# A row-sum kernel's first load as two partition halves, issued by SyncE and ScalarE at the program's entry

## The chip, the cores and the metric

The kernel runs on one core of a Trainium2 chip. Times are device microseconds of one execution, without the profiler unless a text says "in its trace". Profiles come from one profiled execution, whose span runs from the first to the last instruction.

## The reference

The input is 67 MB of float32, and each row of 1024 numbers is summed.

```python
def setup_inputs():
    batch, seq, dim = 32, 512, 1024
    return {"x": np.random.randn(batch, seq, dim).astype(np.float32)}

def reference(x):
    return np.sum(x, axis=-1).astype(np.float32)
```

## The kernel before

The 16,384 rows are cut into eight groups of 16 rows for each of the 128 partitions. A group is 8.4 MB, 64 KB per partition, and is loaded into one of three buffers. SyncE issues all loads, so they stand in one queue (q1 of the page below, 67.12 MB). VectorE (DVE) sums the rows as they land. At the end ScalarE (ACT) helps with some of them. The first group is cut in two, 4 rows and 12 rows, so that DVE gets work early, and the first load is moved in front of the entry barrier. These are the parts that matter here:

```python
def issue_first_load_at_entry(nc):
    main, *rest = nc.main_func.blocks
    SP = mybir.EngineType.SP
    for block in rest:
        insts = list(block.instructions)
        at = next((k for k, i in enumerate(insts)
                   if isinstance(i, mybir.InstDMACopy) and i.engine == SP), None)
        if at is None:
            continue
        load = insts.pop(at)
        assert not load.sync_info.on_wait
        block.instructions = insts
        entry = list(main.instructions)
        k = next(k for k, i in enumerate(entry)
                 if isinstance(i, mybir.InstDrain) and i.engine == SP)
        main.instructions = entry[:k] + [load] + entry[k:]
        return

# ... (cut)
FIRST = 4
# ...
def rows(t, a, n, j, n_act):
    nv = n - n_act
    block = t[:, a * dim : (a + n) * dim].rearrange("p (n d) -> p n d", d=dim)
    load = nc.sync.dma_start(out=block, in_=rows_from(j, n))
    if nv:
        sums_of.append(vec(sums[:, j : j + nv], block[:, :nv, :]))
    # ... (cut: ScalarE's rows)
    return load

for g in range(last):
    t = inpool.tile([P, BIG * dim + 4], fp32)
    if g == 0:
        rows(t, 0, FIRST, 0, 0)
        first = sums_of[-1]
        rows(t, FIRST, BIG - FIRST, FIRST, 0)
        continue
    load = rows(t, 0, BIG, g * BIG, BIG // 2 if g == last - 1 else 0)
    if g == 1:
        hold(load, first, "no descriptors of later loads while the first ones start")
```

## Time and profile before

| | before |
|---|---|
| time, median of the 6 runs made beside the changed kernel | 162.57 us (162.22 to 163.04) |
| span of the profiled run | 160.4 us |
| first issue on SyncE | 0.00 to 0.38 us |
| first reduce starts | 7.19 us |
| 12-row reduce starts | 21.72 us |
| distance of the 16-row reduces | 19.35 us |
| first of the last row's three pieces landed (DVE waits for it; the last piece landed at 157.61) | 156.89 us |

The profile page of the kernel before has these lines: the span, each engine's busy time, and the load queue q1 with its packets, megabytes and share of sixteen DMA engines' time.

```profile
span 160.4 us, 125 instructions
...
DVE 121.1 (76%) x17; ACT 18.5 (12%) x33; POOL 0.2 (0%) x4
...
q1 hardware_dynamic: 2304, 67.12, 97.4%
```

The load stream is busy for nearly the whole span and DVE is not. The timeline of DVE shows the same. Its columns are start, duration, engine, line, operation, names, shapes, count, and in brackets the idle time before it and what ended it.

```profile
7.19 4.42 DVE L98 TENSOR_REDUCE sums<-t 128x4 f32<-128x4096 f32 x1 [7.19 <-DMA t<-in_x_dram]
21.72 12.95 DVE L98 TENSOR_REDUCE sums<-t 128x12 f32<-128x12288 f32 x1 [10.11 <-DMA t<-in_x_dram]
41.07 17.22 DVE L98 TENSOR_REDUCE sums<-t 128x16 f32<-128x16384 f32 x1 [6.40 <-DMA t<-in_x_dram]
60.42 17.22 DVE L98 TENSOR_REDUCE sums<-t 128x16 f32<-128x16384 f32 x1 [2.13 <-DMA t<-in_x_dram]
79.78 17.22 DVE L98 TENSOR_REDUCE sums<-t 128x16 f32<-128x16384 f32 x1 [2.14 <-DMA t<-in_x_dram]
99.13 17.22 DVE L98 TENSOR_REDUCE sums<-t 128x16 f32<-128x16384 f32 x1 [2.13 <-DMA t<-in_x_dram]
```

A 16-row reduce takes 17.22 us, and then DVE stands still for 2.1 us until the next load lands. The loads set the pace: 8.39 MB in 19.35 us is 433 GB/s.

The timeline of the entry shows SyncE's first two issues:

```profile
0.00 0.38 SPq L137 DMA_DIRECT2D t<-in_x_dram  x1
...
0.79 0.33 SPq L137 DMA_DIRECT2D t<-in_x_dram  x1
```

In the windows view, a row is a stretch: its length, the busy time of DVE, ACT and POOL, the clock, the mean busy share of the DMA engines, and GB/s. A packet counts where it starts, so short windows are uneven, and a share can exceed 1.

```profile
2.00:6.00 4.00, 0.00 (x0) 0.07 (x1) 0.00 (x0) 1.00 0.99 422
```

In this stretch all sixteen DMA engines are busy and move 422 GB/s. The trace also records every DMA packet, with its start, duration, size and queue but without its engine. The first load is 128 packets of 16 KB, so eight for each of sixteen engines if they are shared out evenly (at 3, 4 and 5 us sixteen are in flight). The first fourteen, started up to 1.32 us, take 0.94 to 1.43 us; from 2.4 us on, a packet takes 0.61 us (one of them 0.70).

### The profile page before, as it was taken

How to read it: one execution, taken by the hardware profiler on the slowest of the kernel's cores; microseconds unless marked ns; L12 is line 12 of the kernel's file. 1: busy time of each engine (PE TensorE's matmuls, PEld its weight loads, DVE VectorE, ACT ScalarE, POOL GpSimd, SP SyncE). 2: the span in 40 equal slices, each digit the busy share in tenths (PEclk: the TensorE clock that was granted, in tenths of full speed). 3: DMA queues.
4: the chain of work that ended last, by engine and by line, in shares of the span. 5: the costliest groups of instructions: out<-in, count | busy, mean ns of one | idle time of the engine just before them, and what ended most of it. 6: DMA issues, size and time to landing. Idle time of an engine off the chain costs nothing.

```text
span 160.4 us, 125 instructions
## 1 busy us (share of the span) xinstructions
DVE 121.1 (76%) x17; ACT 18.5 (12%) x33; POOL 0.2 (0%) x4
## 2 busy tenths in 40 slices
DVE  0280059960799959999499994999949998697882
ACT  3000000000000000000000000000000000696882
POOL 0000000000000000000000000000000000000000
DMA  7999996996996996996996996996999989999992
GB/s 261 458 466 515 392 523 261 523 523 261 523 523 261 523 523 261 523 523 261 523 523 261 523 523 262 523 490 294 523 392 392 523 360 425 392 425 425 407 399 61
DMA packets 3216, 67.18 MB, mean 419 GB/s; under 512 B 1296, under 2 KB 1680, under 8 KB 1808
## 3 DMA queue, kind: packets, MB, share of 16 engines
q1 hardware_dynamic: 2304, 67.12, 97.4%
q10 hardware_dynamic: 912, 0.06, 0.3%
HBM read 67.11 MB, written 0.07 MB: 419 GB/s over the span
## 4 chain that ended last, share of the span: by engine, by line
DMA 72%; DVE 25%; SPq 1%; issue 0%; DVEq 0%
DMA t<-in_x_dram 72%; DVE sums L98 24%; SPq L137 1%; DVE t L112 1%; DVEq L112 0%; DVEq L214 0%
## 5 line engine op out<-in xcount | busy, mean ns | idle before, releaser
L98 DVE TENSOR_REDUCE sums<-t 128x16 f32<-128x16384 f32 (+5 forms) x11 | 120.1, 10917 | 36.1 <-DMA t<-in_x_dram 36.1
L125 ACT ACTIVATE unread<-t 128x1024 f32<-128x1024 f32 x16 | 16.2, 1012 | 138.2 <-DMA t<-in_x_dram 138.2
L125 ACT ACTIVATION_READ_ACCUMULATOR unread<-t 128x1 f32 x16 | 3.0, 186 | 0.0
L112 DVE CUSTOM_DVE_ANT_0 t<-t 128x241 f32<-128x241 f32 (+2 forms) x3 | 1.0, 339 | 0.9 <-DMA t<-in_x_dram 0.7
L125 ACT ACT_TABLE_LOAD x1 | 1.3, 1283 | 0.8 <-PEq L203 0.8
L112 DVE DVE_READ_ACCUMULATOR2_ANT t<- 128x1 f32 x2 | 0.2, 84 | 0.0
L203 POOL MEMSET const-bfloat16-1.0<- 128x1 bf16 x1 | 0.1, 102 | 0.0
L203 POOL MEMSET const-uint8-127<- 128x1 uint8 x1 | 0.1, 102 | 0.0
L203 POOL MEMSET const-float32-0.0<- 128x1 f32 x1 | 0.1, 100 | 0.2 <-issue 0.2
L203 POOL MEMSET const-float32-1.0<- 128x1 f32 x1 | 0.1, 99 | 0.0
L112 DVE DVE_READ_ACCUMULATOR2_ANT sums<- 128x1 f32 x1 | 0.1, 83 | 0.0
## 6 DMA issues: line engine op xcount, KB each, us to landing
t<-in_x_dram SPq DMA_DIRECT2D x1, 6144.0 KB, 20.9
t<-in_x_dram SPq DMA_DIRECT2D x2, 2048.0 KB, 21.4
t<-in_x_dram SPq DMA_DIRECT2D x1, 4096.0 KB, 31.2
t<-in_x_dram SPq DMA_DIRECT2D x1, 1024.0 KB, 37.7
t<-in_x_dram SPq DMA_DIRECT2D x1, 512.0 KB, 38.5
t<-in_x_dram SPq DMA_DIRECT2D x1, 241.0 KB, 38.6
t<-in_x_dram SPq DMA_DIRECT2D x1, 144.0 KB, 38.6
t<-in_x_dram SPq DMA_DIRECT2D x1, 127.0 KB, 38.3
```

The source lines that it names most:

```text
L98: return nc.vector.tensor_reduce(out=dst, in_=src, axis=mybir.AxisListType.X, op=mybir.AluOpType.add)
L112: return nc.vector.tensor_tensor_reduce(out=src[:, :n], in0=src[:, :n], in1=src[:, n:], scale=1.0, scalar=0.0, op0=mybir.AluOpType.add, op ...
L125: nc.scalar.activation(out=unread[:, :n], in_=src, func=mybir.ActivationFunctionType.Copy, accum_out=dst,)
L137: load = nc.sync.dma_start(out=block, in_=rows_from(j, n))
L203: nc = _bacc.Bacc("TRN2", target_bir_lowering=False, num_devices=1)
```

## The change

The intent is to start the stream sooner: two queues each take half of the first load at the program's entry, instead of one queue taking all of it. Partitions 0 to 63 go to SyncE, partitions 64 to 127 to ScalarE.

```diff
+def issue_first_loads_at_entry(nc):
+    for engine in (mybir.EngineType.SP, mybir.EngineType.Activation):
+        issue_first_load_at_entry(nc, engine)
+
-def issue_first_load_at_entry(nc):
+def issue_first_load_at_entry(nc, SP):
     main, *rest = nc.main_func.blocks
-    SP = mybir.EngineType.SP
@@
-    nc.at_finalize(issue_first_load_at_entry)
+    nc.at_finalize(issue_first_loads_at_entry)
@@ def rows(t, a, n, j, n_act):
-            load = nc.sync.dma_start(out=block, in_=rows_from(j, n))
+            if j == 0:
+                half = P // 2
+                for eng, p0 in ((nc.sync, 0), (nc.scalar, half)):
+                    load = eng.dma_start(
+                        out=block[p0 : p0 + half], in_=rows_from(j, n)[p0 : p0 + half]
+                    )
+            else:
+                load = nc.sync.dma_start(out=block, in_=rows_from(j, n))
```

## The prediction

> **What bounds the kernel now.** The load stream. The page gives 67.11 MB read in a span of 160.4 us, queue q1 busy for 97.4% of sixteen engines' span; DVE is busy 76%, ACT 12%. The chain of waits is 72% DMA t<-in_x_dram. In the timeline the 16-row reduces start every 19.35 us (41.07, 60.42, 79.78, 99.13, 118.49), so 8.39 MB per 19.35 us = 433 GB/s, and DVE idles 2.1 us before each. All 67.11 MB at that rate is 155 us; the last load lands at 156.9. So only some 2 us in front of the stream and 3.5 us behind it are not bandwidth. The front: SyncE's first issue is 0.00 to 0.38, the first packets start at about 1.0 (windows view), the first reduce starts at 7.19. 2.10 MB at 433 GB/s is 4.84 us, so the stream starts, in effect, at 2.35.

> **What the change does.** The first load (2048 KB, 4 rows) becomes two of 64 partitions, one on each queue. Removed: at most part of SyncE's 0.38 us issue (estimate 0.05 to 0.15, later issues take 0.33) and perhaps some of the spread of the engines' first packets (first starts lie between 1.0 and 1.6). Added: one issue on ScalarE (its store's issue took 0.41), before its table load at 0.79; ScalarE first works on data at 137.8, so that is free. The second load's issue (0.79) may slip by 0.1 to 0.2 us; its packets are wanted only at 6.4. The first reduce waits for two semaphores. All else stays. Since the stream never runs dry afterwards, the end moves by exactly what the stream gains or loses in its first 10 us.

> **The gain** is at most 0.3 us (0.2%): after its first packet each engine is already at full rate[...].

> **The danger** is the shape. [...] Nothing in this trace shows it yet. [...] up to twice 4.84 us for the first 2.1 MB, a loss of up to 4.8 us. [...] I take a mean loss of about 1.3 us, and expect no gain over 0.5 us.

> **Predicted time:** 163.8 us, 8 in 10 between 162.2 and 167.3. Faster by over 2%: 0.01; within 2%: 0.72; slower by over 2%: 0.27.

> **What would show it.** The first reduce's start: 7.0 to 7.4 [...], 8.5 to 12 if not. The windows view between 2 and 7 us: about 430 GB/s, or 220 to 350. The start of the 12-row reduce (21.72) and of the 16-row ones, all shifted by one constant equal to the change of span; DVE's idle time before each 16-row reduce still 2.1 us. The span behind the last load unchanged at about 3.5 us.

> **What would make it wrong.** The low half finishing first, so that 48 KB packets of the second load delay the high half: it moves the first reduce, not the end.  [...] A shift that grows along the kernel would contradict me.

In "What would show it" the condition was that the halves cost nothing. About 162.5 us for the kernel before and a mean loss of 1.3 us came to 163.8 us, and with the worst loss, 4.8 us, it came to the range's upper end of 167.3. The 1.3 us was the guess between no loss and 4.8 us. The 4.8 us are the trace's 4.84 us for the first 2.10 MB, taken once more. That a half would take twice as long was the assumption: no run had measured it when the prediction was made, and the result below has 225 GB/s against 422. What the trace shows of "already at full rate" is the 0.61 us of the packets from 2.4 us on.

## The result, and the profile after

The changed kernel takes 168.40 us (6 runs, 167.97 to 169.22) against 162.57 us before. The ratio is 1.0362, with a 95% interval of 1.0328 to 1.0396: slower by 5.8 us. Ratios here are the mean time of one kernel's fast runs over that of the other's fast runs in the same rounds, so they are not quite the ratios of the medians. The predicted time was 163.8 us, with a range up to 167.3 us.

The page of the changed kernel:

```profile
span 167.1 us, 128 instructions
...
DVE 121.1 (72%) x17; ACT 18.5 (11%) x33; POOL 0.2 (0%) x4
...
q1 hardware_dynamic: 2240, 66.07, 94.6%
q10 hardware_dynamic: 992, 1.11, 3.1%
```

DVE's busy time is the same, so no compute was added. The timeline of DVE:

```profile
19.41 4.42 DVE L103 TENSOR_REDUCE sums<-t 128x4 f32<-128x4096 f32 x1 [19.41 <-DMA t<-in_x_dram]
28.49 12.95 DVE L103 TENSOR_REDUCE sums<-t 128x12 f32<-128x12288 f32 x1 [4.66 <-DMA t<-in_x_dram]
47.85 17.22 DVE L103 TENSOR_REDUCE sums<-t 128x16 f32<-128x16384 f32 x1 [6.41 <-DMA t<-in_x_dram]
67.20 17.22 DVE L103 TENSOR_REDUCE sums<-t 128x16 f32<-128x16384 f32 x1 [2.13 <-DMA t<-in_x_dram]
86.56 17.22 DVE L103 TENSOR_REDUCE sums<-t 128x16 f32<-128x16384 f32 x1 [2.13 <-DMA t<-in_x_dram]
105.91 17.22 DVE L103 TENSOR_REDUCE sums<-t 128x16 f32<-128x16384 f32 x1 [2.13 <-DMA t<-in_x_dram]
```

The 12-row reduce starts 6.77 us later (28.49 against 21.72). Every 16-row reduce is later by the same 6.8 us, with the same 2.13 us of idle time before most of them. All of the loss therefore arises before the second load lands, and none of it is won back. The profiled runs differ by 6.7 us, a little more than the medians' 5.8 us: the profiled run was one of the longer runs of the changed kernel (168.92 us).

The entry in the timeline:

```profile
0.00 0.55 SPq L145 DMA_DIRECT2D t<-in_x_dram  x1
0.12 0.54 ACTq L145 DMA_DIRECT2D t<-in_x_dram  x1
...
1.47 0.35 SPq L149 DMA_DIRECT2D t<-in_x_dram  x1
```

The two issues do overlap, but neither is shorter. A load of 64 partitions is issued in 0.55 us, where 128 partitions took 0.38. (Over the runs it is 0.52 to 0.60 us for the 64-partition loads, against 0.33 to 0.49 for the 128-partition loads of the kernel before. It isn't their number alone: of mid_straddle's two 32-partition loads, below, the first took 0.34 us and the last 0.58.) The first packets start at 1.33 us instead of 1.01 (packet records). The entry barrier comes behind both issues (SyncE waits 0.5 us there, 0.2 in the kernel before) and lets the second load out at 1.47 instead of 0.79.

The same stretch in the windows view, and the 10 us after it:

```profile
2.00:6.00 4.00, 0.00 (x0) 0.76 (x1) 0.00 (x0) 1.00 1.03 225
8.00:18.00 10.00, 0.00 (x0) 0.00 (x0) 0.00 (x0) 1.00 0.98 283
```

The busy share is 1.03 (before, 0.99), and from 2.3 us on the packet records have 16 packets in flight. So all sixteen DMA engines work, at about half the rate: 225 GB/s against 422. A 16 KB packet now takes 1.27 us instead of 0.61. The low half goes first: the last of its 64 packets starts at 5.50 us, the first of the high half at 5.51. From 7.90 us on the high half takes turns with the second load's 48 KB packets (none of the high half's packets starts between 8.71 and 10.95 us, nor between 12.47 and 14.70). In that stretch both are slow: the high half's 16 KB packets take 1.18 us, the 48 KB packets 2.57 us (medians) instead of 1.82. All 48 packets of the second load that start before the high half is through are slow (2.20 to 3.06 us).

I sum each group's packet durations beyond what the same packets take undisturbed (0.309, 0.611, 1.815 and 2.418 us for 8, 16, 48 and 64 KB, from the trace of the kernel before) and divide by sixteen engines. This gives the loss by part:

| in the trace, us (sums over the whole run, per engine) | before | changed | halves on one queue |
|---|---|---|---|
| first packet starts | 1.01 | 1.33 | 1.34 |
| 16 KB packets on SyncE's queue | 0.58 | 2.33 | 4.96 |
| 16 KB packets on ScalarE's queue | none | 2.13 | none |
| 48 KB packets of the second load | 0.00 | 2.36 | 0.40 |
| last load packet ends | 157.11 | 163.87 | 162.57 |

For the changed kernel the sum is 0.32 + 1.75 + 2.13 + 2.36 = 6.56 us of the 6.76 us by which its last load packet ends later.

### The profile page after: what moved, and what is told of

It reads as the page before. It is cut to its first block, busy times and chain, and to the rows that moved or that the text cites. A ratio compares the mean times of both kernels' runs of the same rounds, so it can differ in the third digit from the quotient of the medians.

```text
span 167.1 us, 128 instructions
## 1 busy us (share of the span) xinstructions
DVE 121.1 (72%) x17; ACT 18.5 (11%) x33; POOL 0.2 (0%) x4
## 3 DMA queue, kind: packets, MB, share of 16 engines
HBM read 67.11 MB, written 0.07 MB: 402 GB/s over the span
## 4 chain that ended last, share of the span: by engine, by line
DMA 73%; DVE 24%; SPq 1%; issue 0%; DVEq 0%
DMA t<-in_x_dram 73%; DVE sums L103 23%; SPq L149 1%; DVE t L117 1%; DVEq L117 0%; DVEq L226 0%
```

## The experiments

Two theories were open. The partition theory: the loss lies in which partitions a load has, whoever issues it and whenever; a half like those of the changed kernel moves at half rate (225 GB/s against 422). The recorded texts call it the port theory, after a mechanism that no trace or run shows. The queue theory: the loss lies in ScalarE's issuing at the entry, in two queues taking turns, or in the later barrier. All ten kernels of this section gave correct results. The diffs of rows_two_queues and halves_one_queue are against the changed kernel, that of mid_halves is against the kernel before, and those of mid_alternate and mid_straddle are against mid_halves.

### rows_two_queues: split by rows, not by partitions

Two queues and the entry stay, but each half has all 128 partitions.

```diff
-                half = P // 2
+                half = n // 2
-                        out=block[p0 : p0 + half], in_=rows_from(j, n)[p0 : p0 + half]
+                        out=block[:, p0 : p0 + half, :], in_=rows_from(j, n)[:, p0 : p0 + half, :]
```

> The first load is again two loads, one on each queue at the entry, but each takes 2 of the 4 rows on all 128 partitions. Port theory [...]: near the kernel before, 162.0 to 163.2 us, 16 KB-equivalent service of about 0.6 us per engine, first reduce at 7.0 to 7.9 us. Queue theory (the loss is in ScalarE issuing at the entry, in two queues taking turns, or in the late barrier): near the changed kernel, 167 to 169 us. What the entry alone costs (first packets at 1.3 instead of 1.0 us) shows here as 0.3 us.

Measured: 162.61 us, ratio 1.0004 (0.9985 to 1.0022, 6 runs). Two queues at the entry cost nothing, and they gain nothing either: the first packets start at 0.99 us, against 1.01 with one issue. So the 0.3 us that were expected from the entry did not appear. A second expectation missed, the start of the first reduce:

```profile
14.59 4.42 DVE L103 TENSOR_REDUCE sums<-t 128x4 f32<-128x4096 f32 x1 [14.59 <-DMA t<-in_x_dram]
21.86 12.95 DVE L103 TENSOR_REDUCE sums<-t 128x12 f32<-128x12288 f32 x1 [2.85 <-DMA t<-in_x_dram]
41.23 17.22 DVE L103 TENSOR_REDUCE sums<-t 128x16 f32<-128x16384 f32 x1 [6.41 <-DMA t<-in_x_dram]
```

The first reduce starts at 14.59 us, not near 7, since ScalarE's 8 KB packets take turns with the second load's 48 KB packets, which begin between 5 and 6 us (windows view: packets of 999 GB/s start there, against 401 to 426 in each of the three microseconds before). The turns themselves cost nothing here: every 48 KB packet keeps its 1.815 us, and the 8 KB packets their 0.309. The 12-row reduce moves by 0.14 us only, so the end doesn't move. The first reduce's start is not a measure of the loss; that of the second is.

### halves_one_queue: both halves issued by SyncE

```diff
-    for engine in (mybir.EngineType.SP, mybir.EngineType.Activation):
+    for engine in (mybir.EngineType.SP, mybir.EngineType.SP):
-                for eng, p0 in ((nc.sync, 0), (nc.scalar, half)):
+                for eng, p0 in ((nc.sync, 0), (nc.sync, half)):
```

> The same two partition halves, but both issued by SyncE, so one queue and no turns between queues. Port theory: 2.1 MB at half of 433 GB/s, so a loss of 4.84 us against before: 167.0 to 168.0 us, packets of 16 KB taking 1.2 us through both halves, first reduce at about 12; the second load's 48 KB packets at 1.8 us from their start, since nothing of the halves is left to mix with them. Queue theory: 162.3 to 163.3 us. The rest of the changed kernel's loss (6.8 us in its trace against 4.8) is then the mixing of the high half with the second load and the later start.

Measured: 167.66 us, ratio 1.0313 (1.0288 to 1.0337, 4 runs), so about 5.2 us lost with one queue.

```profile
2.00:6.00 4.00, 0.00 (x0) 1.12 (x1) 0.00 (x0) 1.00 0.90 197
```

The 16 KB packets take 1.275 us (median of the halves). Eight of them in place of eight undisturbed ones would cost 8 x (1.275 - 0.611) = 5.3 us. An exact doubling would cost 4.9, so in a half a packet runs at a little less than half the rate. The table's sums give less, 4.96 - 0.58 = 4.38 us, since the first packets are slow in both kernels (0.94 to 1.43 us in the kernel before). The late first packets are here too (1.34 us) without ScalarE: they came with the 64-partition issues (1.32 to 1.34 us in this run, the changed kernel and alternate_first2, against 0.99 to 1.01 with 128 partitions). The 48 KB packets lose only 0.40 us. What the changed kernel loses beyond this one, some 0.7 us by the medians, comes with the second queue: the high half then takes turns with the second load.

### mid_halves: the halves in the middle of the stream

The entry is that of the kernel before. The load of the fourth group is two halves on SyncE's queue. (The recorded texts call it the fourth 16-row load. It is the third: the first group comes as 4 and 12 rows.)

```diff
+            if j == 3 * BIG:
+                half = P // 2
+                for p0 in (0, half):
+                    load = nc.sync.dma_start(
+                        out=block[p0 : p0 + half], in_=rows_from(j, n)[p0 : p0 + half]
+                    )
+            else:
+                load = nc.sync.dma_start(out=block, in_=rows_from(j, n))
```

> The entry is that of the kernel before. The fourth 16-row load (8.4 MB, in the middle of the stream) is two partition halves on SyncE's queue. Port theory: this load alone takes twice 19.35 us, so plus 19.4 us: about 182 us, with all of it in the idle time before one reduce. A theory of the entry (late start, cold queues, descriptors) or of two queues: no change, 162 to 163.5 us.

Measured: 183.95 us, ratio 1.1318 (2 runs).

```profile
61.24 17.22 DVE L98 TENSOR_REDUCE sums<-t 128x16 f32<-128x16384 f32 x1 [2.83 <-DMA t<-in_x_dram]
101.61 17.22 DVE L98 TENSOR_REDUCE sums<-t 128x16 f32<-128x16384 f32 x1 [23.15 <-DMA t<-in_x_dram]
120.79 17.22 DVE L98 TENSOR_REDUCE sums<-t 128x16 f32<-128x16384 f32 x1 [1.95 <-DMA t<-in_x_dram]
```

The load arrives 23.15 us after DVE is ready for it, where 2.13 was usual. Its 64 KB packets take 5.12 us (median) against 2.42, and 8 x (5.12 - 2.42) = 21.6 us is the measured loss, 2.2 us more than the doubling that was expected: the factor per packet is 2.12, so a half moves at a little less than half the rate. It has nothing to do with the entry, with ScalarE or with a second queue.

### mid_alternate: even and odd partitions

Same place, same queue, same 64 partitions per load, but every second one.

```diff
-                for p0 in (0, half):
+                for p0 in (0, 1):
-                        out=block[p0 : p0 + half], in_=rows_from(j, n)[p0 : p0 + half]
+                        out=block[p0::2], in_=rows_from(j, n)[p0::2]
```

> As mid_halves, but the two loads take the even and the odd partitions[...]. [...] 162 to 164 us. [...] half rate again, up to about 182 us, unless the engines fall out of step.

The first figure is for the case that such a split costs nothing, the second for half rate again.

Measured: 162.51 us, ratio 0.9999 (0.9966 to 1.0032, 2 runs).

```profile
60.46 17.22 DVE L98 TENSOR_REDUCE sums<-t 128x16 f32<-128x16384 f32 x1 [2.13 <-DMA t<-in_x_dram]
79.89 17.22 DVE L98 TENSOR_REDUCE sums<-t 128x16 f32<-128x16384 f32 x1 [2.21 <-DMA t<-in_x_dram]
99.18 17.22 DVE L98 TENSOR_REDUCE sums<-t 128x16 f32<-128x16384 f32 x1 [2.06 <-DMA t<-in_x_dram]
```

Every packet of this load takes 2.42 us, and none is longer than 2.44; in mid_halves it was 5.12. It is not the number of partitions or packets in a load, but which partitions they are. My second figure, half rate again, did not come true. The trace doesn't have which engine writes which partition, so it can't say why, nor whether the recorded exception, engines out of step, had a part in it.

### mid_straddle: partitions 0 to 31, 32 to 95, 96 to 127

```diff
-                for p0 in (0, half):
+                for p0, p1 in ((0, 32), (32, 96), (96, 128)):
-                        out=block[p0 : p0 + half], in_=rows_from(j, n)[p0 : p0 + half]
+                        out=block[p0:p1], in_=rows_from(j, n)[p0:p1]
```

> As mid_halves, all on SyncE's queue, but the fourth 16-row load is three loads of partitions 0 to 31, 32 to 95 and 96 to 127. [...] the 64 partitions 32 to 95 run at full rate, packets of 64 KB at 2.42 us, and only the two outer quarters at half, at 5.1 us: plus 8 packets' worth of bytes per engine halved, so plus 10.8 us, about 173.2 us. If any 64 neighbouring partitions are slow [...]: plus 21.6 us as in mid_halves, 184 us. If it were the number of partitions, quarters would be slower than halves: over 184 us.

What is left to test is whether it matters that a load has partitions on both sides of 64.

Measured: 173.12 us, ratio 1.0651 (2 runs). The windows of the three loads, in order:

```profile
59.50:69.00 9.50, 8.21 (x1) 0.00 (x0) 0.00 (x0) 1.00 1.03 221
69.00:79.30 10.30, 9.02 (x1) 0.00 (x0) 0.00 (x0) 1.00 0.98 407
79.30:89.00 9.70, 0.00 (x0) 0.00 (x0) 0.00 (x0) 1.00 1.02 216
```

One rival is left. In every run a partition reads the same rows of the input, so a load from one side of 64 also reads one contiguous half of a group's 8.4 MB. No run gives a half other rows, so none tells the writing side from the reading side. Which of the two sides it is was not shown.

### after_first2, before_first2: half the bytes

The changed kernel and the kernel before, each with this edit:

```diff
-    FIRST = 4
+    FIRST = 2
```

> The changed kernel with a first load of 2 rows in place of 4, so half the bytes in the two partition halves. Port theory: the loss is in proportion to these bytes, apart from the 0.3 us later start: half of the changed kernel's 5.8 us plus a little, 165.2 to 166.3 us. A fixed cost of the split or of two queues at the entry: still 168 us.

> The reference for the first-load-of-2-rows runs: the kernel before with that size alone changed. Both theories: 162 to 163.2 us, as the stream never runs dry.

Measured: 164.70 us (4 runs) and 162.55 us (2 runs), so 2.15 us lost where the 4-row first load lost 5.8. The loss went with the bytes and was no fixed cost, but it fell to less than half, below what I expected. In the packet records the high half is nearly done (last packet starts at 6.02 us) when the second load's packets begin (5.44 to 6.63 us). So the second load's packets lose only 0.58 us, against 2.36 in the changed kernel.

### alternate_first2, alternate_first4 and halves_own_buffer: a split at the entry by even and odd partitions

These have the changed kernel's two queues at the entry and 64 partitions per load, but SyncE takes the even partitions and ScalarE the odd ones. The first load gets a buffer of its own, meant to keep the second load from waiting for it; the second load is issued at 1.48 us, as in the changed kernel (1.47). No run shows whether it would wait without. The control halves_own_buffer has that buffer too, but the low and the high half.

```diff
-                        out=block[p0 : p0 + half], in_=rows_from(j, n)[p0 : p0 + half]
+                        out=block[p0 // half :: 2], in_=rows_from(j, n)[p0 // half :: 2]
@@ alternate_first4 and halves_own_buffer (alternate_first2: a tile of 2 rows beside "sums")
                 first = sums_of[-1]
+                t = inpool.tile([P, BIG * dim + 4], fp32)
                 rows(t, FIRST, BIG - FIRST, FIRST, 0)
```

> As after_first2 (two queues at the entry, 64 partitions each, 2 rows) but SyncE takes the even partitions and ScalarE the odd ones, into a tile of its own, so that the second load needs no wait. Port theory: no loss but the late start, 162.3 to 163.3 us. If it is 64-partition loads or two queues as such: as after_first2.

> The changed kernel with the same bytes on the same two queues at the entry, 64 partitions each, but even partitions on SyncE and odd ones on ScalarE, in a buffer of their own so that the second load needs no wait (the buffers turn by one place more; no load waits longer for that). Port theory: packets of 16 KB at 0.61 us on both queues; what remains is the later first packets (1.3 instead of 1.0 us), since the first load's 4.8 us now cover the later second issue: 162.5 to 163.1 us. In alternate_first2 the cover was 2.4 us and 1.2 us were lost. Queue theory: 168 us.

> The control for alternate_first4: the same own buffer and the same two queues, but the low and the high half as in the changed kernel. Both theories: as the changed kernel, 167.8 to 169.3 us. Anything else would mean that the own buffer matters.

| first load | queues at the entry | partitions | us | ratio to before |
|---|---|---|---|---|
| 2 rows | two | even, odd | 163.62 (4 runs) | 1.0071 (1.0043 to 1.0099) |
| 4 rows | two | even, odd | 163.03 (6 runs) | 1.0013 (0.9989 to 1.0037) |
| 4 rows, own buffer | two | low, high | 168.88 (4 runs) | 1.0394 (1.0365 to 1.0423) |

The last two kernels differ in one line and by 5.9 us. With 4 rows the even-odd split is at the kernel before's time; its 16 KB packets take 0.61 us on both queues. With 2 rows it loses 1.1 us, more than expected. There the first packets start 0.32 us later (1.32 against 1.00), and three of the sixteen first packets of the second load take 2.68 to 3.09 us instead of 2.12. A second load that is issued at 1.48 instead of 0.79 us and has only half the cover could explain it; that is my guess, and no run isolates this. In the profiled run of alternate_first4, 89 of the 64 KB packets, started between 26 and 71 us, took 2.50 to 2.65 instead of 2.42 us. I can't explain those, and its ratio rests on the timed runs.

No kernel beats the kernel before. The nearest, rows_two_queues, is the same within its interval.

## Why the prediction was wrong

- **What bounds the kernel** was right: the load stream sets the end, and the shift of the 16-row reduces is one constant. The span behind the wait that the prediction took for the last load's is 3.5 us in both traces (160.4 - 156.9 and 167.1 - 163.6). That wait is for the first of the last row's three pieces.
- **The gain** of "at most 0.3 us" was nil. The issue was not shortened by "0.05 to 0.15" but lengthened by 0.17 us, and the first packets came 0.32 us later. Even where the issue was shorter (0.36 us in rows_two_queues), the first packets started no earlier than 0.99 us.
- **The danger** was named rightly as the shape, and the rate was right: "220 to 350" GB/s was predicted for the bad case and 225 measured for a half, against 407 GB/s for partitions 32 to 95. The mechanism that the prediction gave was not shown.
- **The step that failed is "I take a mean loss of about 1.3 us".** It was a guess between no loss and the worst case, with no trace or run behind it. The packet records show nothing that softened the loss. The packets did not start together: twelve started between 1.33 and 1.60 us, the next at 2.02 and later. But the low half's packets all came first, and until 5.51 us no packet for the other side had started. Once the first packets are through, each 16 KB packet of the low half takes about 1.27 us. In place of 1.3 us the loss was 5.8.
- **"A loss of up to 4.8 us" was too low as well.** Not for the halves' own packets: their excess over the kernel before is 1.75 + 2.13 = 3.88 us. But the start is 0.32 us later, and the estimate ended at the first 2.1 MB, while the high half also slowed the second load's packets, whose excess is 2.36 us of the trace's 6.6. The prediction had these turns only as something that "moves the first reduce, not the end". That is so for the row split (14.59 us and no loss), but not for a half. The second load has all 128 partitions, and of its packets none of the 48 that started beside the high half kept 1.82 us (2.20 to 3.06). How the turns slow a whole load was not shown.
- **The first reduce** at "8.5 to 12 if not" came at 19.41, for these turns.
- **The second load's issue** slipped by 0.69 us instead of "0.1 to 0.2". With a first load of 4 rows this costs next to nothing (alternate_first4, ratio 1.0013, has the same slip).

## What to carry to other kernels

In this case a load could be split along the free dimension (rows_two_queues, ratio 1.0004), or by partitions so that each part had as many below partition 64 as above: even and odd ones (mid_alternate, 0.9999, and alternate_first4, 1.0013, though 1.0071 with the smaller first load of alternate_first2), and 32 to 95, which moved at 407 GB/s. A part that lay on one side moved at about half rate (225 GB/s against 422), and it slowed another load that ran beside it (48 KB packets took 2.57 us against 1.82). No other kernel or layout was tried, so measure it there. Where the load stream is the bound as here, a shift of 6.8 us early was a shift of 6.8 us at the end. So I estimate that a first load issued 0.1 us sooner is worth at most 0.1 us. Look first at where the first packet really starts: here, with all 128 partitions, it started at 1.0 us whether one queue or two had issued it. Before splitting, ask which wait the split would shorten, and cost the worst case through every load that runs beside the changed one, not for the changed load alone.
